# Where four small projections stand: first products with their results kept in DRAM, or last products beside the gate

## The chip, the cores and the metric

The kernel runs on one core of a Trainium2 chip. The metric is the device time of one execution in microseconds (us), the median of several runs. Within a core, TensorE (PE) multiplies, VectorE (DVE), ScalarE (ACT) and GpSimd (POOL) do elementwise work, and SyncE (SP) and ScalarE issue the DMAs used here. Each engine takes its instructions in the order in which they were built.

## The reference

One layer of a hybrid decoder block over 256 tokens and 2048 features, in float32:

```python
h = rmsnorm(x, norm_mix_g)
u = h @ w_in                       # 12288 columns in ten parts
ya = b * conv3(c * xa) * silu(za)  # short convolution, 1024 wide
yb = hgrn2(q, f, iv) * silu(og)    # gated linear recurrence, 1024 wide
m = sigmoid(ga) * (ya @ w_a_out) + sigmoid(gb) * (yb @ w_b_out)
x = x + m @ w_o
gate = sigmoid(rmsnorm(x, ple_norm_g) @ w_ple_gate)
x = x + gate * (p @ w_ple_proj)    # p: 256 tokens x 256, w_ple_proj: 256 x 2048
return rmsnorm(x, final_norm_g)
```

The term `p @ w_ple_proj` depends on inputs alone, so it can be computed at any time before the last sum.

## The kernel before, in words

**Products.** Every float32 operand is split into a high and a low part (`hi` is the value in the matmul's format, `lo = value - hi`), and every product is three matmuls: high by high, high by low, low by high (`product`, L842 to L844). The weights stream in as chunks of 128 x 1024 (512 KB), one chunk per *step*. A step is two k-blocks by two token halves by three matmuls, so 12 matmuls of 512 columns. `split(pos)` makes one step's high part on ScalarE (L119, tile `whi`) and low part on VectorE (L120, `wlo`). Activations are put into their high and low parts by `put` (L156 and L157: `xh`, `xl`).

**Groups.** Steps are gathered in groups by output columns (512 at a time): 24 groups of `w_in` (eight steps each), A and B (four steps each, after each `gb`), O0 to O3 (`w_o`, eight steps) and PG0 to PG3 (`w_pg`, eight steps). The projection of p is PP0 to PP3 (`w_pp`, one step each). Before, PP0 and PP1 stand between O3 and PG0, PP2 follows PG0, and PP3 follows PG1. PG3 is written out apart, at the end, in three pieces.

**PSUM.** `bank("g")` has four banks in rotation and each group takes two, so a group can begin when the epilogue of the group two before it has read its banks.

**Epilogues.** Each group has a generator (`ep_f`, `ep_o`, `ep_pp`, `ep_pg` and so on) that runs in pieces: `advance()` runs every active one up to its next `yield`, once per step. `ep_o` adds the product to x, turns the result (from tokens by features to features by tokens) through DRAM (`turned`: four DMAs out, one back, a transpose on VectorE), and puts it as the operand `x1T` of the PG groups. `ep_pp` copies its two banks to a tile `pw` (L612, ScalarE), which `ep_pg` multiplies with the gate.

**Order.** Two things set it: the main loop over `steps`, which splits weights three steps ahead (`ahead`, `LEAD`) and loads four more (`AHEAD`); and a scheduler that, when the kernel is built, orders each engine's instructions from that program. `tc.issue_after` and `tc.keep_in_program_order` bind it. Raw weights have three buffers of two steps each (`raw`, bufs=3), and split weights four (`wp`), with six more in a pool `late` from PG0 on. Nearly all DMAs are issued on SyncE's queue in order; a DMA that waits holds up those behind it. Eight DMAs may be under way; the next waits for the landing of the one eight before.

**Start.** x comes in transposed as eight pieces (`xT`, 256 KB), between the first six weight chunks, all on SyncE's queue; `prm` (36 KB of gains) is on ScalarE's. Eight warm-up matmuls on a zeroed tile run before the first product.

Of the kernel before, what the change touches and what calls it, by code (L numbers as in the profile page):

```python
# [15 lines left out]
P = 128  # L16
# [7 lines left out]
CW = 512  # L24
PLE = 256
EPS = 1e-6
WARM = 8
LB_FLOOR = 1e-30
LB_MAX = 1.0 - 1e-6
SCAN = 64  # L30
# [14 lines left out]
def hybrid_kernel(ctx, tc, xT, x, pT, prm, gfin, masks, w_in, w_a, w_b, w_o, w_pg, w_pp, out):  # L45
# [28 lines left out]
    def nm(s):  # L74
        uid[0] += 1
        return f"{s}_{uid[0]}"

    def t4(tag="t4", bufs=None):
        bufs = bufs or {"tmp1": 8, "tmp2": 5, "tmp3": 5}[state["tmp"]]
        return pools[state["tmp"]].tile([P, 1024], F32, tag=tag, bufs=bufs, name=nm(tag))  # L80
# [12 lines left out]

    def load(pos):
        w, g, c = stream[pos]
        nch = w.shape[2]
        key = (id(w), g, c // 2)
        if key not in loaded:
            raw = wp.tile([P, 2, 2 * CW], F32, tag="raw", bufs=3, name=nm("raw"))
            loaded[key] = raw  # L100
            if nch == 1 or FIRST <= pos < FIRST + 4:
                for i in range(min(nch, 2)):
                    nc.sync.dma_start(out=raw[:, i, :], in_=w[g, :, c + i, :])
            elif pos >= FIRST:
                nc.sync.dma_start(out=raw, in_=w[g, :, c : c + 2, :])
        return loaded[key]

    def split(pos, halves=(0, 1)):
        w, g, c = stream[pos]
        src = load(pos)[:, c % 2, :]  # L110

        pool, n = (pools["late"], 6) if (pos - state.get("late", len(steps))) % 10 < 6 and "late" in state else (wp, 4)
        if pos not in parts:
            parts[pos] = tuple(
                pool.tile([P, 2 * CW], F32R, tag=tag, bufs=n, name=nm(tag)) for tag in ("whi", "wlo")
            )
        hi, lo = parts[pos]
        s = slice(halves[0] * CW, (halves[-1] + 1) * CW)
        a = nc.scalar.activation(out=hi[:, s], in_=src[:, s], func=AF.Copy)  # L119
        v = nc.vector.tensor_tensor(  # L120
            out=lo[:, s], in0=src[:, s], in1=hi[:, s].bitcast(F32), op=ALU.subtract
        )
        state["splits"] = (a.ins, v.ins)


    prm_t = const.tile([P, PRM_N], F32, name="prm_t")
    nc.scalar.dma_start(out=prm_t, in_=prm)

    if PAD_CONST:
        nc.gpsimd.memset(const.tile([P, PAD_CONST], F32, name="pad"), 0.0)  # L130
# [14 lines left out]
    def operand(pool, tag, n):  # L145

        return tuple(pool.tile([P, n, T], F32R, tag=tag + x, bufs=1, name=nm(tag + x)) for x in "hl")
# [459 lines left out]
            state["rstd2"] = rsqrt_of(tot, NT, D, "r2")  # L607

    def ep_pp(j, psum):
        pw = t4("pw", 2)  # L610
        for t in range(NT):
            nc.scalar.activation(out=pw[:, t * CW : (t + 1) * CW], in_=psum[t], func=AF.Copy)  # L612
        state["pw", j] = pw
        yield

    def ep_pg(j, psum):
        xs, pw, gt = state["x"], state["pw", j], t4()
# [63 lines left out]
        "f": ep_f, "q": ep_q, "iv": ep_iv, "og": ep_og, "c": ep_c, "xa": ep_xa, "za": ep_za, "b": ep_b,  # L681
        "ga": ep_ga, "gb": ep_gb, "A": ep_a, "B": ep_bb, "O": ep_o, "PG": ep_pg, "PP": ep_pp,
    }
    groups = []
    for n, (kind, j) in enumerate(IN_ORDER):
        groups.append((kind, j, w_in, n, "hT"))
        if kind == "gb":
            groups.append(("A", j, w_a, j, "yaT"))
            groups.append(("B", j, w_b, j, "ybT"))
    groups += [("O", j, w_o, j, "mT") for j in range(4)]  # L690
    groups.append(("PP", 0, w_pp, 0, "pT"))
    for j in range(4):
        if j < 3:
            groups.append(("PP", j + 1, w_pp, j + 1, "pT"))
        groups.append(("PG", j, w_pg, j, "x1T"))
    steps = []
    active, done = [], 0
    for gi, (kind, j, w, g, op) in enumerate(groups):
        for c in range(w.shape[2]):
            stream.append((w, g, c))  # L700
            steps.append((gi, c))

    last_group = len(steps) - w_pg.shape[2]


    state["hT"] = operand(big, "x", KT)
    LEAD, AHEAD = 3, 4
    TOKENS, NORM = 6, 10
    FIRST = 6
    xraw = [t4() for _ in range(4)]  # L710
    for c in range(KT // 2):
        n = 2 * (c % 2)
        nc.sync.dma_start(
            out=xraw[c // 2].rearrange("p (k t) -> p k t", k=4)[:, n : n + 2, :],
            in_=xT[:, 2 * c : 2 * c + 2, :],
        )
        if c < FIRST:
            raw, w = load(c)[:, c % 2, :], stream[c][0][0, :, c, :]
            for s in (slice(0, CW), slice(CW, 2 * CW)) if c == 0 else (slice(0, 2 * CW),):
                nc.sync.dma_start(out=raw[:, s], in_=w[:, s])  # L720


    warm = pools["tmp1"].tile([P, 4, P], F32, tag="both", bufs=1, name="warm")
    nc.vector.memset(warm, 0.0)
    warm = warm.rearrange("p h t -> p (h t)").bitcast(mybir.dt.bfloat16)[:, :CW]
    wb = bank("s")
    for _ in range(WARM):
        nc.tensor.matmul(wb, warm[:, :P], warm, start=True, stop=True)
# [64 lines left out]
        g = state["gfin"] = pools["tmp3"].tile([P, D], F32, name="gfin_t")  # L793
        nc.sync.dma_start(out=g, in_=gfin.partition_broadcast(P))

    def load_p():
        pr = t4()[:, : 2 * T]
        nc.sync.dma_start(out=pr.rearrange("p (k t) -> p k t", k=2), in_=pT)
        state["pT"] = operand(pools["tmp3"], "p", 2)
        hi, lo = (v.rearrange("p k t -> p (k t)") for v in state["pT"])  # L800
        nc.scalar.activation(out=hi, in_=pr, func=AF.Copy)
        nc.vector.tensor_tensor(out=lo, in0=pr, in1=hi.bitcast(F32), op=ALU.subtract)

    def third_part():

# [8 lines left out]
        state["ss3"] = sc(12, "ss3", 1)  # L814
        nc.gpsimd.memset(state["ss3"].rearrange("p (t j) -> p t j", t=NT)[:, :, 5:6], EPS)

    def step(e, free=False):

        with ExitStack() as order:
            for i in state["splits"] if done < len(steps) and not free else ():  # L820
                order.enter_context(tc.issue_after(i))
            try:
                next(e)
            except StopIteration:
                active.remove(e)
# [10 lines left out]

        return LEAD + min(max(pos - (last_group - 20), 0) // 4, 5)

    def product(psum, op, k, t, hi, lo, first, last):

        oh, ol = (x[:, k, t * P : (t + 1) * P] for x in op)
        nc.tensor.matmul(psum, oh, hi, start=first, stop=False)  # L842
        nc.tensor.matmul(psum, oh, lo, start=False, stop=False)  # L843
        nc.tensor.matmul(psum, ol, hi, start=False, stop=last)  # L844

    psum = None
    for pos, (gi, c) in enumerate(steps[:last_group]):
        kind, j, w, g, opname = groups[gi]
        nch = w.shape[2]
        if kind == "PG" and j == 0 and c == 0:  # L850
            close_pool("m")
            open_pool("late", "left")
            state["late"] = done
        while done < min(pos + 1 + ahead(pos), len(steps)):
            if done < 2:
                for i in range(2):
                    put_x(2 * done + i)
                    split(done, (i,))
            else:
                for k in range(2 * done, min(2 * done + 2, KT)):  # L860
                    put_x(k)
                split(done)
            done += 1
        if pos == 4:
            begin()
        if 0 <= pos - NORM < 4:
            add_squares(pos - NORM)
        if pos == NORM + 3:
            norm_of_x()
        if pos == NORM + 4:  # L870
            active.append(ep_f(0, waiting))
            step(active[-1])
            nc.sync.dma_start(out=mask_t, in_=masks)
        if c == 0:
            psum = [bank("g") for _ in range(NT)]
        hi, lo = parts.pop(pos)
        for i in range(2):
            k = 2 * c + i
            s = slice(i * CW, (i + 1) * CW)
            for t in range(NT):  # L880
                product(psum[t], state[opname], k, t, hi[:, s], lo[:, s], k == 0, k == 2 * nch - 1)


        if kind == "PP":
            advance()
        for q in range(done, min(done + AHEAD, len(steps)) if pos >= FIRST else 0):
            load(q)
        if 0 <= pos - TOKENS < 4:
            load_tokens(pos - TOKENS)
        if kind != "PP":  # L890
            advance()
        if kind == "O" and j == 0 and c == nch - 3:
            finish()
            third_part()
        if kind == "O" and j > 0 and c == 1:
            residual(j)
        if kind == "O" and j in (1, 2) and c == 4:
            (load_p, load_gfin)[j - 1]()
        if c == nch - 1:
            if kind == "f" and j == 0:  # L900

                waiting = psum
                for n in ("yaT", "ybT"):
                    state[n] = operand(pools["branch"], n, DC // P)
            if kind == "ga" and j == 0:
                finish()
                second_part()
            if kind == "O" and j == 0:
                state["x1T"] = operand(big, "x", KT)
            if kind == "f" and j == 0:  # L910
                continue
            active.append(epilogues[kind](j, psum))
            step(active[-1], kind == "O" and j == 3)

# [94 lines left out]
```

## Time and profile before

| | |
|---|---|
| time, median of 3 runs (lowest to highest) | 836.47 us (836.06 to 836.76) |
| the profiled execution's own time | 836.98 us |
| its span, first to last instruction | 835.2 us |
| TensorE busy (matmuls) | 822.8 us, 99% of the span |
| TensorE weight loads | 684.1 us, 82% |
| VectorE busy | 529.3 us, 63% |
| ScalarE busy | 434.2 us, 52% |
| GpSimd busy | 91.9 us, 11% |
| DMA | 183.01 MB, mean 219 GB/s |
| first product of the program | 6.2 us after the span's start |

The profile shows one execution. Times within it are counted from the span's start. A timeline row gives start, duration, engine, line, operation, output and inputs, and in brackets the idle time of the engine before it and what ended that. TensorE's matmuls overlap their neighbours, so their spacing from start to start tells their rate, not their duration. The row of a stretch gives, behind the busy times of five engines, the granted clock of TensorE, the busy share of the DMA engines and the GB/s.

### The profile page before, as it was taken

The page shows a single profiled execution, that of the slowest core. Times are in us where ns is not written, and L with a number is a line of the kernel's source. Part 1 is how long each engine was busy: PE and PEld are TensorE (multiplying, and loading weights), DVE is VectorE, ACT ScalarE, POOL GpSimd, SP SyncE. Part 2 cuts the span into 40 slices and gives each one's busy share as a digit, 9 for nine tenths or more (in the row PEclk, how much of TensorE's full clock was granted, in tenths as well). Part 3 has the DMA queues.
Part 4 walks back from the last instruction along what each step waited for, and adds up shares of the span by engine and source line. Part 5 has one row for each costly group of instructions (what it writes and reads, how often), then busy time and mean ns, then how long its engine had stood idle before and what let it go on. Part 6 is the DMA issues. An engine that isn't in the chain of part 4 may idle for free.

```text
span 835.2 us, 9807 instructions
## 1 busy us (share of the span) xinstructions
PE 822.8 (99%) x3752; PEld 684.1 (82%) x3752; DVE 529.3 (63%) x600; ACT 434.2 (52%) x563; POOL 91.9 (11%) x76
## 2 busy tenths in 40 slices
PE   8999999999999999999999999999999999999995
PEld 6888888888888888888888888888888888878885
DVE  6557678777684687777655455545546566576722
ACT  7566654545564654545544443543543555475623
POOL 1000054100000153100001001001001000001110
PEclk9999999999999999999999999999999999999998
DMA  9977554747775555648656556655655888685702
GB/s 330 368 238 259 197 182 175 235 166 245 260 249 202 179 177 184 217 151 296 207 188 228 195 196 232 221 188 186 236 196 182 301 272 303 222 320 216 261 1 101
DMA packets 39792, 183.01 MB, mean 219 GB/s; under 512 B 4544, under 2 KB 13760, under 8 KB 21824
## 3 DMA queue, kind: packets, MB, share of 16 engines
q1 hardware_dynamic: 39312, 181.81, 62.8%
q8 instruction: 29, 0.48, 0.2%
q10 hardware_dynamic: 432, 0.56, 0.2%
q14 instruction: 19, 0.16, 0.1%
HBM read 170.82 MB, written 11.53 MB: 218 GB/s over the span
## 4 chain that ended last, share of the span: by engine, by line
PE 96%; issue 1%; ACT 1%; DVE 0%; DMA 0%; POOLq 0%; POOL 0%; DVEq 0%; ACTq 0%
PE g L842 31%; PE g L844 31%; PE g L843 31%; PE s L328 1%; DMA prm_t<-in_prm 0%; PE s L437 0%; PE s L450 0%; PE s L449 0%; PE s L448 0%; ACT whi L119 0%; ACT xs L663 0%; ACT t L593 0%; DVE wlo L120 0%; DVE xl L157 0%; ACT t L646 0%
## 5 line engine op out<-in xcount | busy, mean ns | idle before, releaser
L120 DVE TENSOR_TENSOR wlo<-raw,whi 128x1024 fp32r<-128x1024 f32 (+1 forms) x294 | 361.5, 1234 | 258.5 <-ACT whi L119 257.6
L119 ACT ACTIVATE whi<-raw 128x1024 fp32r<-128x1024 f32 (+1 forms) x294 | 308.1, 1053 | 340.8 <-PE g L844 292.3
L842 PE MATMUL g<-whi,xh 128*128 128x512 f32 (+1 forms) x912 | 353.0, 388 | 2.0 <-ACT whi L119 1.2
L843 PE MATMUL g<-wlo,xh 128*128 128x512 f32 (+1 forms) x912 | 352.2, 386 | 0.0
L844 PE MATMUL g<-whi,xl 128*128 128x512 f32 (+1 forms) x912 | 352.0, 386 | 0.0
L842 PEld LDWEIGHTS g<-whi,xh 128*128 128x128 f32 x912 | 171.8, 189 | 37.2 <-ACT whi L119 2.1
L844 PEld LDWEIGHTS g<-whi,xl 128*128 128x128 f32 x912 | 171.7, 188 | 34.4
L843 PEld LDWEIGHTS g<-wlo,xh 128*128 128x128 f32 x912 | 171.9, 188 | 34.1 <-DVE wlo L120 0.2
L843 PE MATMUL g<-wlo,mh 128*128 128x512 f32 x128 | 49.6, 389 | 0.0
L842 PE MATMUL g<-whi,mh 128*128 128x512 f32 x128 | 49.5, 389 | 0.0
L844 PE MATMUL g<-whi,ml 128*128 128x512 f32 x128 | 49.5, 389 | 0.0
L573 POOL TENSOR_TENSOR t<-ga,gb 128x512 f32<-128x512 f32 x8 | 14.1, 1787 | 249.1 <-DVE gb L569 249.1
L842 PEld LDWEIGHTS g<-whi,mh 128*128 128x128 f32 x128 | 24.0, 188 | 5.0
L843 PEld LDWEIGHTS g<-wlo,mh 128*128 128x128 f32 x128 | 24.0, 188 | 5.0
L374 POOL TENSOR_TENSOR t<-b 128x512 f32<-128x512 f32 x10 | 20.9, 2086 | 65.3 <-DMA raw<-in_w_in 33.6
L844 PEld LDWEIGHTS g<-whi,ml 128*128 128x128 f32 x128 | 24.0, 188 | 4.9
L356 POOL TENSOR_TENSOR X<-t,kT 128x256 f32<-128x256 f32 x12 | 14.1, 1177 | 99.4 <-ACT t L370 57.7
L842 PE MATMUL g<-whi,yaTh 128*128 128x512 f32 x64 | 24.9, 389 | 0.0
L843 PE MATMUL g<-wlo,yaTh 128*128 128x512 f32 x64 | 24.9, 389 | 0.0
L844 PE MATMUL g<-whi,yaTl 128*128 128x512 f32 x64 | 24.9, 389 | 0.0
L842 PE MATMUL g<-whi,ybTh 128*128 128x512 f32 x64 | 24.9, 389 | 0.0
L843 PE MATMUL g<-wlo,ybTh 128*128 128x512 f32 x64 | 24.9, 389 | 0.0
(148 smaller groups left out, 555.9 us busy)
## 6 DMA issues: line engine op xcount, KB each, us to landing
raw<-in_w_in SPq DMA_DIRECT2D x91, 1024.0 KB, 4.9
raw<-in_w_o SPq DMA_DIRECT2D x16, 1024.0 KB, 6.5
raw<-in_w_pg SPq DMA_DIRECT2D x16, 1024.0 KB, 5.5
turn<-t SPq DMA_DIRECT2D x72, 128.0 KB, 2.8
t<-turn SPq DMA_DIRECT2D x18, 512.0 KB, 5.3
raw<-in_w_a SPq DMA_DIRECT2D x8, 1024.0 KB, 4.9
raw<-in_w_b SPq DMA_DIRECT2D x8, 1024.0 KB, 5.0
raw<-in_w_in SPq DMA_DIRECT2D x9, 512.0 KB, 7.8
```

Source lines behind the costliest of these rows:

```text
L119: a = nc.scalar.activation(out=hi[:, s], in_=src[:, s], func=AF.Copy)
L120: v = nc.vector.tensor_tensor(out=lo[:, s], in0=src[:, s], in1=hi[:, s].bitcast(F32), op=ALU.subtract)
L328: nc.tensor.matmul(bk[:, s], X[:, 0, h, :], X[:, 1, h, :], start=True, stop=True)
L356: eng.tensor_tensor(out=xv[:, w, :, :, half, :], in0=ev[:, :, blk, :, half, :], in1=src[:, :, blk, :, half, :], op=ALU.mult,)
L374: nc.gpsimd.tensor_tensor(out=er, in0=br, in1=ref, op=ALU.subtract)
L573: nc.gpsimd.tensor_tensor(out=spread(m, t), in0=blocks(ga[:, s]), in1=blocks(gb[:, s]), op=ALU.add)
L842: nc.tensor.matmul(psum, oh, hi, start=first, stop=False)
L843: nc.tensor.matmul(psum, oh, lo, start=False, stop=False)
L844: nc.tensor.matmul(psum, ol, hi, start=False, stop=last)
```

## The change

The four PP groups become the first groups of the program. Their operand p is loaded first, on SyncE's queue, while the first `w_pp` chunk comes in two halves on ScalarE's queue. `prm` moves to SyncE's queue. p is put by VectorE alone (`put_p`), into the memory that `yaT` takes later. `ep_pp` copies its banks and writes the copy to DRAM (`kept`); `load_projection` reads it back into `pw` during each PG group. The step-and-group list is now made at the top, the raw buffers are shared by pairs of steps (`pos // 2`), the first step's products are in an order of their own, there are ten warm-up matmuls on a tile zeroed to half the width, the token loads and the norm of x move by two positions, and the exemption of O3's first epilogue piece from `issue_after` goes.

```diff
-WARM = 8
+WARM = 10
...
+    def load_first(pos, eng, pieces):
+        w, g, c = stream[pos]
+        for i in range(pieces):
+            s = slice(i * (2 * CW // pieces), (i + 1) * (2 * CW // pieces))
+            eng.dma_start(out=load(pos)[:, pos % 2, s], in_=w[g, :, c, s])
...
+    groups += [("PP", j, w_pp, j, "pT") for j in range(4)]
     for n, (kind, j) in enumerate(IN_ORDER):
...
-    groups.append(("PP", 0, w_pp, 0, "pT"))
-    for j in range(4):
-        if j < 3:
-            groups.append(("PP", j + 1, w_pp, j + 1, "pT"))
-        groups.append(("PG", j, w_pg, j, "x1T"))
+    groups += [("PG", j, w_pg, j, "x1T") for j in range(4)]
...
-    TOKENS, NORM = 6, 10
+    TOKENS, NORM = 8, 12
...
+    load_first(0, nc.scalar, 2)
+    praw = t4()[:, : 2 * T]
+    nc.sync.dma_start(out=praw.rearrange("p (k t) -> p k t", k=2), in_=pT)
+    load_first(1, nc.sync, 1)
     prm_t = const.tile([P, PRM_N], F32, name="prm_t")
-    nc.scalar.dma_start(out=prm_t, in_=prm)
+    nc.sync.dma_start(out=prm_t, in_=prm)
...
     def ep_pp(j, psum):
-        pw = t4("pw", 2)
+        pw, d = t4(), dram.tile([P, 1024], F32, tag="kept", bufs=4, name=nm("kept"))
         for t in range(NT):
             nc.scalar.activation(out=pw[:, t * CW : (t + 1) * CW], in_=psum[t], func=AF.Copy)
-        state["pw", j] = pw
+        state["kept", j] = d
         yield
+        yield
+        nc.sync.dma_start(out=d, in_=pw)
...
     for c in range(KT // 2):
+        if c + 2 < FIRST:
+            load_first(c + 2, nc.sync, 1)
         ... one piece of xT, nc.sync ...
-        if c < FIRST:
-            ... one w_in chunk, nc.sync ...
...
+    def put_p(k):
+        hi, lo = (z[:, k, :] for z in state["pT"])
+        src = praw[:, k * T : (k + 1) * T]
+        nc.vector.tensor_copy(out=hi, in_=src)
+        nc.vector.tensor_tensor(out=lo, in0=src, in1=hi.bitcast(F32), op=ALU.subtract)
+
+    def load_projection(j):
+        pw = state["pw", j] = t4("pw", 2)
+        nc.sync.dma_start(out=pw, in_=state["kept", j])
...
-            if done < 2:
+            if done == 0:
                 for i in range(2):
-                    put_x(2 * done + i)
+                    put_p(i)
                     split(done, (i,))
             else:
-                for k in range(2 * done, min(2 * done + 2, KT)):
+                for k in range(2 * (done - 4), min(2 * (done - 4) + 2, KT)) if done >= 4 else ():
                     put_x(k)
                 split(done)
...
+            for n in ((0,), (2,), (1,)) if pos == 0 and i == 0 else ((0, 1, 2),):
+                for t in range(NT):
+                    product(psum[t], state[opname], k, t, hi[:, s], lo[:, s], k == 0, k == 2 * nch - 1, n)
...
+        if kind == "PG" and c == 4:
+            load_projection(j)
+            if j == 2:
+                load_projection(3)
...
-            step(active[-1], kind == "O" and j == 3)
+            step(active[-1])
```

More of the change, by code (lines that the diff above doesn't have):

```diff
@@ L95, in load @@
         w, g, c = stream[pos]
-        nch = w.shape[2]
-        key = (id(w), g, c // 2)
-        if key not in loaded:
+        if pos // 2 not in loaded:
             raw = wp.tile([P, 2, 2 * CW], F32, tag="raw", bufs=3, name=nm("raw"))
-            loaded[key] = raw
-            if nch == 1 or FIRST <= pos < FIRST + 4:
-                for i in range(min(nch, 2)):
+            loaded[pos // 2] = raw
+            if FIRST <= pos < FIRST + 4:
+                for i in range(2):
                     nc.sync.dma_start(out=raw[:, i, :], in_=w[g, :, c + i, :])
@@ L105, in load @@
                 nc.sync.dma_start(out=raw, in_=w[g, :, c : c + 2, :])
-        return loaded[key]
+        return loaded[pos // 2]
+    def load_first(pos, eng, pieces):
[3 more added lines that the diff above has]
+            eng.dma_start(out=load(pos)[:, pos % 2, s], in_=w[g, :, c, s])
     def split(pos, halves=(0, 1)):
         w, g, c = stream[pos]
-        src = load(pos)[:, c % 2, :]
+        src = load(pos)[:, pos % 2, :]
         pool, n = (pools["late"], 6) if (pos - state.get("late", len(steps))) % 10 < 6 and "late" in state else (wp, 4)
@@ L123, in split @@
         state["splits"] = (a.ins, v.ins)
+    groups = []
+    groups += [("PP", j, w_pp, j, "pT") for j in range(4)]
+    for n, (kind, j) in enumerate(IN_ORDER):
+        groups.append((kind, j, w_in, n, "hT"))
+        if kind == "gb":
+            groups.append(("A", j, w_a, j, "yaT"))
+            groups.append(("B", j, w_b, j, "ybT"))
+    groups += [("O", j, w_o, j, "mT") for j in range(4)]
+    groups += [("PG", j, w_pg, j, "x1T") for j in range(4)]
+    steps = []
+    active, done = [], 0
+    for gi, (kind, j, w, g, op) in enumerate(groups):
+        for c in range(w.shape[2]):
+            stream.append((w, g, c))
+            steps.append((gi, c))
+    last_group = len(steps) - w_pg.shape[2]
+    LEAD, AHEAD = 3, 4
+    TOKENS, NORM = 8, 12
+    FIRST = 6
+    load_first(0, nc.scalar, 2)
+    praw = t4()[:, : 2 * T]
+    nc.sync.dma_start(out=praw.rearrange("p (k t) -> p k t", k=2), in_=pT)
+    load_first(1, nc.sync, 1)
     prm_t = const.tile([P, PRM_N], F32, name="prm_t")
-    nc.scalar.dma_start(out=prm_t, in_=prm)
+    nc.sync.dma_start(out=prm_t, in_=prm)
     if PAD_CONST:
@@ L683, in hybrid_kernel @@
     }
[L684 to L690, printed above, removed]
-    groups.append(("PP", 0, w_pp, 0, "pT"))
-    for j in range(4):
-        if j < 3:
-            groups.append(("PP", j + 1, w_pp, j + 1, "pT"))
-        groups.append(("PG", j, w_pg, j, "x1T"))
[L696 to L703, printed above, removed]
     state["hT"] = operand(big, "x", KT)
-    LEAD, AHEAD = 3, 4
-    TOKENS, NORM = 6, 10
-    FIRST = 6
+    for n in ("yaT", "ybT"):
+        state[n] = operand(pools["branch"], n, DC // P)
+    state["pT"] = tuple(z[:, :2, :] for z in state["yaT"])
     xraw = [t4() for _ in range(4)]
     for c in range(KT // 2):
+        if c + 2 < FIRST:
+            load_first(c + 2, nc.sync, 1)
         n = 2 * (c % 2)
@@ L716, in hybrid_kernel @@
         )
-        if c < FIRST:
-            raw, w = load(c)[:, c % 2, :], stream[c][0][0, :, c, :]
-            for s in (slice(0, CW), slice(CW, 2 * CW)) if c == 0 else (slice(0, 2 * CW),):
-                nc.sync.dma_start(out=raw[:, s], in_=w[:, s])
     warm = pools["tmp1"].tile([P, 4, P], F32, tag="both", bufs=1, name="warm")
-    nc.vector.memset(warm, 0.0)
-    warm = warm.rearrange("p h t -> p (h t)").bitcast(mybir.dt.bfloat16)[:, :CW]
+    nc.vector.memset(warm[:, :2, :], 0.0)
+    warm = warm[:, :2, :].rearrange("p h t -> p (h t)").bitcast(mybir.dt.bfloat16)
     wb = bank("s")
@@ L794, in load_gfin @@
         nc.sync.dma_start(out=g, in_=gfin.partition_broadcast(P))
[L796 to L802, printed above, removed]
+    def put_p(k):
[6 more added lines that the diff above has]
+        nc.sync.dma_start(out=pw, in_=state["kept", j])
     def third_part():
@@ L815, in third_part, with step @@
         nc.gpsimd.memset(state["ss3"].rearrange("p (t j) -> p t j", t=NT)[:, :, 5:6], EPS)
-    def step(e, free=False):
+    def step(e):
         with ExitStack() as order:
-            for i in state["splits"] if done < len(steps) and not free else ():
+            for i in state["splits"] if done < len(steps) else ():
                 order.enter_context(tc.issue_after(i))
@@ L837, in ahead, with product @@
         return LEAD + min(max(pos - (last_group - 20), 0) // 4, 5)
-    def product(psum, op, k, t, hi, lo, first, last):
+    def product(psum, op, k, t, hi, lo, first, last, which=(0, 1, 2)):
         oh, ol = (x[:, k, t * P : (t + 1) * P] for x in op)
-        nc.tensor.matmul(psum, oh, hi, start=first, stop=False)
-        nc.tensor.matmul(psum, oh, lo, start=False, stop=False)
-        nc.tensor.matmul(psum, ol, hi, start=False, stop=last)
+        for n in which:
+            a, b = ((oh, hi), (oh, lo), (ol, hi))[n]
+            nc.tensor.matmul(psum, a, b, start=first and n == 0, stop=last and n == 2)
     psum = None
@@ L879, in hybrid_kernel @@
             s = slice(i * CW, (i + 1) * CW)
-            for t in range(NT):
-                product(psum[t], state[opname], k, t, hi[:, s], lo[:, s], k == 0, k == 2 * nch - 1)
-        if kind == "PP":
+            for n in ((0,), (2,), (1,)) if pos == 0 and i == 0 else ((0, 1, 2),):
+                for t in range(NT):
+                    product(psum[t], state[opname], k, t, hi[:, s], lo[:, s], k == 0, k == 2 * nch - 1, n)
+        if kind == "PG" and j == 0 and c < 2:
             advance()
@@ L889, in hybrid_kernel @@
             load_tokens(pos - TOKENS)
-        if kind != "PP":
+        if kind != "PG" or j or c >= 2:
             advance()
@@ L896, in hybrid_kernel @@
             residual(j)
-        if kind == "O" and j in (1, 2) and c == 4:
-            (load_p, load_gfin)[j - 1]()
+        if kind == "O" and j == 2 and c == 4:
+            load_gfin()
+        if kind == "PG" and c == 4:
+            load_projection(j)
+            if j == 2:
+                load_projection(3)
         if c == nch - 1:
@@ L902, in hybrid_kernel @@
                 waiting = psum
-                for n in ("yaT", "ybT"):
-                    state[n] = operand(pools["branch"], n, DC // P)
             if kind == "ga" and j == 0:
```

## The prediction

> **What bounds it now.** I read the page first, then the timelines of the two places that the change touches, the start and the seam between the group O3 and the group PG0.
>
> ```profile
> span 835.2 us, 9807 instructions
> PE 96%; issue 1%; ACT 1%; DVE 0%; DMA 0%; POOLq 0%; POOL 0%; DVEq 0%; ACTq 0%
> ```
>
> The chain that ended last is TensorE for 96%, so the time is the number of products times their spacing, plus what TensorE waits. The change keeps every product. Only waits and the slow first products can move.
>
> ```profile
> 6.22 1.22 PE L842 MATMUL g<-whi,xh 128*128 128x512 f32 x2 [1.17 <-ACT whi L119]
> 10.23 0.57 PE L842 MATMUL g<-whi,xh 128*128 128x512 f32 x1
> 10.63 0.40 PE L843 MATMUL g<-wlo,xh 128*128 128x512 f32 x1
> 13.63 0.39 PE L844 MATMUL g<-whi,xl 128*128 128x512 f32 x1
> 13.85 0.62 PE L842 MATMUL g<-whi,xh 128*128 128x512 f32 x2
> ```
>
> This is TensorE's timeline at the start. Products begin at 6.22. The first ten stand 0.43 us apart (to 10.23), the others 0.227 (13.63 to 13.85). A step has 12 products, so the 25th product, the first of step 2, starts at 13.85. From there TensorE runs without a break to the seam. So the question at the front is: when does the 25th product start afterwards?
>
> ```profile
> 731.66 0.39 PE L844 MATMUL g<-whi,pl 128*128 128x512 f32 x1
> 732.91 0.50 PE L842 MATMUL g<-whi,xh 128*128 128x512 f32 x1 [0.87 <-ACT pw L612]
> ...
> 732.29 1.06 ACT L612 ACTIVATE pw<-g 128x512 f32<-128x512 f32 x2
> 735.15 2.97 ACT L119 ACTIVATE whi<-raw 128x1024 fp32r<-128x1024 f32 x3
> ```
>
> The seam, TensorE then ScalarE. PG0 starts 1.25 us after the last product of PP1 instead of 0.23: 1.02 us lost. It waits for ScalarE to copy PP0's result out of PSUM, because tag "g" has four banks and every group takes two. This wait is the key to the forecast: two PP groups fill all four banks, and the third user must wait for a copy.
>
> **The front: gain that cannot arrive.** The first products need p (256 KB) and half a w_pp chunk (256 KB), the same bytes as now (x, w_in), but issued at once on two queues instead of 0.44 us apart, and they need no value of prm. VectorE's copy and subtraction of p take the place of ScalarE's 0.91 us. I put the first product at 5.5 to 5.9, so 0.3 to 0.7 us earlier. The shorter memset (0.48 us for 512 columns, now 256) and ten warm-up products of 0.43 us (4.3 us) end near 5.5, so the break before the first product shrinks. At the slow spacing the two steps PP0 and PP1 end by 15.9, and by about 13.3 if the spacing drops at 9 to 10 us, since step 1's weights split near 10.7. All of this is cover for what comes next, and I count it at nothing.
>
> **The front: the new wait.** PP2 (step 2) needs PP0's two banks, so ScalarE's copies at the line `pw[...] <- psum[t]` of ep_pp. In the built order of the changed kernel ScalarE does, in this order: the splits of steps 0 to 3, x's pairs 0 and 1, step 4's split, x's pair 2, step 5's split, and only then the four copies of PP0 and PP1. It is one in-order engine, so PP2 waits for step 5's weights to land. In the built order there are in front of and with those weights: p 256 KB, six weight chunks 3072 KB, three x pieces 768 KB, prm 36 KB: 4132 KB. Before, the same 4132 KB were in when the sixth x piece landed:
>
> ```profile
> 7.42 0.51 SPq L713 DMA_DIRECT2D t<-in_xT  x1
> ...
> t<-in_xT SPq DMA_DIRECT2D x1, 256.0 KB, 8.7
> ```
>
> Issued at 7.42, 8.7 us to landing: 16.1. Then step 5's split (three took 2.97, so 0.99), the copy (1.06 for the pair; alone 0.59, the mean of the eight) and 0.04 to TensorE, as at 732.87 to 732.91: 16.1 + 0.99 + 0.59 + 0.04 = 17.7. The 25th product starts at 17.7 instead of 13.85: **3.9 us lost.** Bounds for the landing: 17.4 (where step 5's weights land now, behind 512 KB more) and 12.4 (4.23 MB at the 410 GB/s of the row below, from 2.0 us on). I take 16.1, since it is the same bytes through the same engines. The Trainium skill, "DMA: Bandwidth & Descriptors", section "Issuing engines are not separate DMA queues", says that queues of several engines share the same 16 DMA engines and that issuing from two saves issue time alone; by it the second queue moves nothing here, as in the sum by equal bytes, and this trace, with prm alone on the second queue, cannot test it.
>
> After 17.7 the front holds. SyncE's queue now has the four `kept` writes (512 KB each) among the weight loads, and each waits for its copy. The worst is step 6 and 7's load behind the first write: issued near 18.7, landed by 24, wanted split by 28.6. Step 8's load is behind the third write (copy near 23.7, after eight pieces of x at 0.43 each): landed near 28, wanted at 34. Step 4 wants PP2's banks at 23.1, copied at 22.8 and 23.7, the second wanted at 23.8. Cost nothing; if this cover were gone, each us late is a us lost.
>
> **The seam.** PP0 and PP1 no longer stand there, so PG0's banks are free and the 1.02 us are **gained**. But the same two groups gave 24 x 0.227 = 5.4 us of cover to O3's way through DRAM: add, copy, turn out, turn back, transpose, put. PG0's 7th step reads what it puts.
>
> ```profile
> 726.54 1.27 DVE L157 SCALAR_TENSOR_TENSOR xl<-t,prm_t,xh 128x256 fp32r<-128x256 f32 x3
> 728.86 0.68 DVE L585 TENSOR_TENSOR xs<-xs,g 128x512 f32<-128x512 f32 x1
> 742.47 1.24 DVE L198 STREAM_TRANSPOSE t<-t 128x1024 f32<-128x1024 f32 x1
> 745.86 1.66 DVE L157 SCALAR_TENSOR_TENSOR xl<-t,prm_t,xh 128x256 fp32r<-128x256 f32 x4
> ```
>
> O3's last product ends at 726.4. If nothing changed, the first low part would be ready at 745.86 + 0.42 = 746.3. PG0 started at 726.4 wants it at 726.4 + 74 x 0.227 = 743.2, so 3.1 us stall. In the built order, however, the second add follows the first at once, no longer behind the puts of O2 and a split (at 726.5 instead of 728.86). ScalarE then makes a split, copy, square, copy (1.04 + 0.63 + 0.80 + 0.63), so the turn goes out at 729.5 instead of 730.2, and one split less stands between transpose and puts (1.2). That makes 746.3 - 0.7 - 1.2 = 744.4: 1.2 stall. The two loads that slowed the turn now are issued earlier; 512 KB of `pw` join them. Both ends 0 and 3.1; I take 0.6, between 0 and 1.2. Net of the seam: -0.4, from -1.0 to +2.1.
>
> **The rest.** Projection weights (2 MB) leave the end and 2 MB of `pw` come back there: the same bytes. The 2 MB written at the front are in spare DMA time after 20 us. The eight copies (4.7 us of ScalarE) leave an end where TensorE waited for them only at the seam. The tail after the last product is unchanged. All nothing.
>
> **Sum:** 3.9 - 0.4 = +3.5 on a span of 835.2: 838.7. The profiled execution took 836.98, 0.51 above the median of the runs, so the median goes from 836.47 to about **840.0**.
>
> **Rivals.**
> (1) *The slow spacing returns.* TensorE idles from about 13.3 to 17.7. The trace shows what idling can do:
>
> ```profile
> 10.60:13.80 3.20, 3.20 (x15) 2.61 (x14) 2.90 (x6) 3.10 (x7) 0.00 (x0) 1.00 1.03 410
> 826.50:829.70 3.20, 0.00 (x0) 0.00 (x0) 1.56 (x5) 1.39 (x4) 0.56 (x1) 1.00 0.00 0
> 829.90:835.00 5.10, 0.00 (x0) 0.00 (x0) 0.40 (x1) 0.58 (x1) 0.00 (x0) 0.50 0.56 207
> ```
>
> These are stretches with the granted clock third from last: 1.00 for 3.4 us after the last product (826.3), 0.50 from 829.8 on. The drop came 3.5 us after the end; the 1.0 us break at the seam left the spacing at 0.23. My break of 4.4 us is longer by 0.9 only, and it shrinks to 1.8 if PP0 and PP1 run at 0.43 throughout (24 products from 5.6, to 15.9); so this is less likely than not. Price: 2.0 us (ten products 0.2 too long, as at the start) to 3.7 (slow from the warm-up at 1.45 to 10.6, 8.0 busy us of 0.43, so 18.7 products); 2.9 in the middle: 842.9. Chance 0.27. The Trainium skill, "TensorE: Matmul & The Clock Gate", section "What's actually happening", has the clock halved after a whole idle window of about 3.4 us, the windows running freely; an estimate from that page is that a break of 4.4 us holds a whole one in about 3 cases of 10. The tail of this trace agrees, with 3.5 us.
> (2) *Not slower: the data come early.* If two queues fill the DMA engines from 2 us on, step 5's weights land at 12.4 and not 16.1; PP2 starts at 14.0, 0.2 late, and the seam gives 1.0: 835.6. The point where it decides is a landing at 13.2. Against it: before, the DMAs ran at 238 GB/s from 5.1 to 6.2 us with work queued, which a second queue does not explain away. Chance 0.12, with landings up to 14.9 (838.1).
> (3) *The seam stalls in full*, 3.1 us, since the latencies of the turn stay: 3.9 - 1.0 + 3.1 = +6.0, 842.5. For it: DMA stays as busy there. Against: the built order drops the work ahead of the second add. Chance 0.12.
>
> **Numbers.** Forecast 0.46 with a range of its own from 838.3 (landing at 15.0, free seam) to 841.6 (landing at 17.0, seam +0.3); rivals 0.27, 0.12, 0.12; 0.03 for anything else. The range 837.5 to 843.7 leaves out most of rival 2 below, and above it the dear end of rivals 1 and 3. What a measurement here tells from no change is about 0.2%, 1.67 us. Slower by more: forecast, rivals 1 and 3: 0.85. Within: nearly all of rival 2, 0.12. Faster by more (below 834.8) needs a landing before 12.4 and a free seam: 0.03.
>
> **What would show it.** TensorE's timeline has a gap of about 4 us before its 25th product, ended by ScalarE's copy in ep_pp, and step 5's split stands right ahead of that copy at 16 to 17 us. Products after it at 0.43 mean rival 1. At the seam the last product of O3 is followed by PG0 within 0.25 us, and any gap lies 16 us later, ended by a put. I am wrong if the 25th product starts before 15, or if the copies run before step 5's weights land.

## The result, and the profile after

| | before | after |
|---|---|---|
| median of 5 runs each, one chip (lowest to highest), us | 836.47 (836.06 to 836.81) | 840.18 (839.48 to 840.42) |
| ratio, 95% interval | | 1.0043 (1.0028 to 1.0057) |
| the profiled execution's own time, its span | 836.98, 835.2 | 840.28, 838.5 |
| the 25th product starts at | 13.85 | 16.37 |
| the last product starts at | 826.04 | 829.72 |

The changed kernel is slower by 3.7 us, close to the forecast (840.0). The parts of that sum, however, are not those of the forecast. First the page of the changed kernel:

```profile
span 838.5 us, 9821 instructions
PE 96%; issue 1%; DMA 1%; ACT 1%; DVE 0%; SPq 0%; POOLq 0%; POOL 0%; ACTq 0%
```

TensorE is still the chain for 96%, so the loss must be in its waits or its spacing. Its timeline at the start (start, duration, operation; in brackets the idle time and what ended it):

```profile
5.24 0.73 PE L859 MATMUL g<-whi,yaTh 128*128 128x512 f32 x2 [0.31 <-DVE yaTl L812]
...
11.86 0.39 PE L859 MATMUL g<-whi,yaTl 128*128 128x512 f32 x1
16.37 0.80 PE L859 MATMUL g<-whi,yaTh 128*128 128x512 f32 x1 [4.12 <-ACT t L643]
16.96 0.63 PE L859 MATMUL g<-wlo,yaTh 128*128 128x512 f32 x1
17.39 0.63 PE L859 MATMUL g<-whi,yaTl 128*128 128x512 f32 x1
...
20.80 0.56 PE L859 MATMUL g<-wlo,yaTh 128*128 128x512 f32 x1
21.20 0.39 PE L859 MATMUL g<-whi,yaTl 128*128 128x512 f32 x1
21.42 0.39 PE L859 MATMUL g<-whi,yaTh 128*128 128x512 f32 x1
```

Two things are to be seen. The 25th product waits 4.12 us for the copy of ep_pp, and starts 2.52 us later than before. And behind the break the products stand 0.43 us apart until 21.20: eleven of them take 4.83 us where 11 x 0.227 = 2.50 would do, another 2.33 us. The rows by stretch (five busy times, granted clock, DMA share, GB/s) say why:

```profile
4.10:10.80 6.70, 5.81 (x23) 3.52 (x22) 5.07 (x9) 4.45 (x7) 0.53 (x1) 1.00 1.02 367
10.90:14.30 3.40, 1.35 (x6) 0.77 (x5) 2.85 (x6) 2.87 (x6) 0.00 (x0) 1.00 1.01 397
14.40:17.70 3.30, 1.33 (x3) 1.14 (x4) 2.69 (x4) 3.21 (x7) 0.00 (x0) 0.50 0.86 322
17.80:21.10 3.30, 3.30 (x9) 2.60 (x8) 2.87 (x7) 3.25 (x8) 0.00 (x0) 0.50 1.00 274
21.20:30.00 8.80, 8.80 (x40) 7.29 (x39) 5.02 (x13) 6.12 (x11) 0.00 (x0) 1.00 0.99 375
```

The granted clock is halved in the middle of the break and comes back at 21.14. What held the copy is in ScalarE's timeline:

```profile
13.79 0.89 ACT L187 ACTIVATE xh<-t,prm_t 128x256 fp32r<-128x256 f32 x2
14.78 1.06 ACT L124 ACTIVATE whi<-raw 128x1024 fp32r<-128x1024 f32 x1
15.74 2.04 ACT L643 ACTIVATE t<-g 128x512 f32<-128x512 f32 x4
```

Step 5's split runs at 14.78, and PP0's copies follow it. The load that it needs was issued at 6.95 and landed 7.7 us later, at 14.67:

```profile
6.95 0.43 SPq L111 DMA_DIRECT2D raw<-in_w_in  x1
...
raw<-in_w_in SPq DMA_DIRECT2D x1, 512.0 KB, 7.7
```

ScalarE itself was busy with the two pieces of x before it until 14.68, so the landing and the engine held the split to the same time. TensorE, then VectorE, at the seam:

```profile
741.94 0.39 PE L859 MATMUL g<-whi,ml 128*128 128x512 f32 x1
742.17 0.39 PE L859 MATMUL g<-whi,xh 128*128 128x512 f32 x1
```

```profile
741.94 1.28 DVE L616 TENSOR_TENSOR xs<-xs,g 128x512 f32<-128x512 f32 x2
...
755.23 1.25 DVE L229 STREAM_TRANSPOSE t<-t 128x1024 f32<-128x1024 f32 x1
756.40 1.18 DVE L125 TENSOR_TENSOR wlo<-raw,whi 128x1024 fp32r<-128x1024 f32 x1
757.51 1.66 DVE L188 SCALAR_TENSOR_TENSOR xl<-t,prm_t,xh 128x256 fp32r<-128x256 f32 x4
```

PG0 follows O3's last product by 0.23 us: the 1.02 us are gained. The first low part of x is there at 757.51 + 0.42 = 757.9, and PG0's 75th product wants it at 742.17 + 74 x 0.227 = 759.0, so nothing stalls.

The spans' difference: +2.52 (the wait), +2.33 (slow products), -1.02 (seam), -0.38 (the tail behind the last product, 8.88 us before and 8.50 after), and -0.15 that small steps leave: +3.30. The medians differ by 3.71, because the profiled execution of the kernel before took 0.51 more than its median and that of the changed kernel 0.10. The start of the kernel before varies: in e6_before_spare_banks (below), which begins with the same instructions, the clock is full at 9.45 instead of 10.59 and the 25th product starts at 13.14 instead of 13.85. So the 2.52 us are counted against a late start of the kernel before.

### The profile page after: what moved, and what is told of

The parts are those of the page before. It is cut to its first block, busy times and chain, and to the rows that moved or that the text cites. A ratio compares the mean times of both kernels' runs of the same rounds, so it can differ in the third digit from the quotient of the medians.

```text
span 838.5 us, 9821 instructions
## 1 busy us (share of the span) xinstructions
PE 823.8 (98%) x3754; PEld 684.2 (82%) x3754; DVE 530.5 (63%) x602; ACT 434.8 (52%) x561; POOL 92.3 (11%) x76
## 4 chain that ended last, share of the span: by engine, by line
PE 96%; issue 1%; DMA 1%; ACT 1%; DVE 0%; SPq 0%; POOLq 0%; POOL 0%; ACTq 0%
PE g L859 93%; PE s L359 1%; DMA raw<-in_w_pp 1%; PE s L468 0%; ACT whi L124 0%; PE s L480 0%; PE s L481 0%; PE s L479 0%; ACT xs L696 0%; DVE wlo L125 0%; ACT t L679 0%; SPq L111 0%; ACT xh L187 0%; DVE t L675 0%; POOLq L1024 0%
## 5 line engine op out<-in xcount | busy, mean ns | idle before, releaser
L859 PE MATMUL g<-whi,yaTh 128*128 128x512 f32 x80 | 32.3, 406 | 4.8 <-ACT t L643 4.1
L859 PE MATMUL g<-wlo,yaTh 128*128 128x512 f32 x80 | 32.1, 403 | 0.2 <-DVE wlo L125 0.2
L859 PE MATMUL g<-whi,yaTl 128*128 128x512 f32 x80 | 31.7, 398 | 0.0
```

Source lines behind the costliest of these rows:

```text
L859: nc.tensor.matmul(psum, a, b, start=first and n == 0, stop=last and n == 2)
```

## The experiments

The theory: PP2 has no free banks, the copy that frees them stands behind step 5's split, and the break this makes also halves the clock. The first rival: the results' way through DRAM, 2.1 MB written at the start and read back at the end, is the cost. The second: the clock is lost for another reason than the break. Times are medians, with lowest to highest; in the same runs the kernel before had 836.43 (e1 to e4), 836.35 (e5 to e8) and 836.76 us (e9 and e10). The end of a label says what the run changes.

### Other banks for PP2 and PP3 (e1_spare_banks)

```diff
-            psum = [bank("g") for _ in range(NT)]
+            psum = [bank("s" if kind == "PP" and j > 1 else "g") for _ in range(NT)]
```

> The changed kernel with PP2 and PP3 in two pairs of the banks of tag s, which nothing else uses so early. Theory A (the loss is PP2's wait for PP0's banks, 2.5 us, and the slow products after the break, 2.3 us): the break before the 25th product goes, it starts near 12.1 instead of 16.4, the spacing stays at 0.23; then step 6 is next to be late, since its weights are still behind the first kept write on SyncE's queue and its split behind nine pieces of x, about 1.7 us. Sum 840.2 - 4.3 - 2.3 + 1.7 = 835.3. Theory B (the loss is the 4 MB of extra DMA traffic): the break may go but the time stays near 840.

Measured: 835.97 us (835.53 to 837.44), ratio to before 0.9995 (0.9986 to 1.0004). The break and the slow products are gone: the 25th product starts at 12.17, and the clock is 1.00 from 4.59 to 830.62. That is 4.20 + 2.33 us, but only 4.2 us of it are left at the end, since new waits have come at steps 6, 8 and 10 (1.1, 0.4 and 0.5 us beyond the spacing, from the starts of the products):

```profile
24.43 0.50 PE L859 MATMUL g<-wlo,xh 128*128 128x512 f32 x1 [0.53 <-DVE wlo L125]
...
36.25 0.50 PE L859 MATMUL g<-wlo,xh 128*128 128x512 f32 x1 [0.18 <-DVE wlo L125]
```

Its SyncE queue shows where these weights were:

```profile
16.50 0.33 SPq L647 DMA_DIRECT2D kept<-t  x1
16.93 1.20 SPq L101 DMA_DIRECT2D raw<-in_w_in  x2
18.22 0.91 SPq L647 DMA_DIRECT2D kept<-t  x2
19.23 1.40 SPq L101 DMA_DIRECT2D raw<-in_w_in  x2
```

The loads of steps 6 to 13 stand behind `kept` writes, which wait for copies. In the changed kernel the same queue costs nothing, because TensorE starts step 6 there 6.4 us later (29.61 against 23.17): one delay covers the other.

### The kept writes on GpSimd's queue as well (e7_writes_apart)

```diff
-        nc.sync.dma_start(out=d, in_=pw)
+        nc.gpsimd.dma_start(out=d, in_=pw)
```

> As e1_spare_banks, with the four kept writes issued on GpSimd's queue instead of SyncE's. e1 came out at 835.97 with waits of 1.3, 0.4 and 0.4 us at steps 6, 8 and 10, whose loads were issued at 16.9 and 19.2 behind kept writes. If the place on SyncE's queue makes these waits, the loads are issued near 12.5 and 15, and the time is 833.9. If the bytes of the writes make them, the waits stay: 835.5 to 836.

Measured: 834.29 us (834.14 to 834.70), ratio 0.9976 (0.9967 to 0.9985). SyncE's queue is now this:

```profile
12.91 2.90 SPq L101 DMA_DIRECT2D raw<-in_w_in  x4
```

The loads go out from 12.91 on, and the waits at steps 6, 8 and 10 are gone. The last product starts at 823.07, 2.13 us earlier than with the spare banks alone: 2.04 of it are the three waits, 0.09 an earlier 25th product (12.08). The medians differ by 1.68 only. In the profiled runs the tail behind the last product makes up for the rest (9.06 us here, 8.49 there). Over the twelve traces this tail is 8.49 to 8.54 in eight and 8.84 to 9.06 in four, and why was not shown.

### Work in the break (e2_fill_break, e8_half_fill)

```diff
+        if kind == "PP" and j == 2:
+            fill = bank("s")
+            for _ in range(FILL):
+                tc.keep_in_program_order(nc.tensor.matmul(fill, warm[:, :P], warm, start=True, stop=True))
```

FILL is 16 in the first and 8 in the second.

> The changed kernel with 16 matmuls on zeros (512 columns, 0.215 to 0.23 us each, 3.6 us together) between PP1 and PP2, so that TensorE is busy in most of the break, and nothing else is changed. Theory A: PP2 starts at 16.4 as before, but the granted clock stays at 1.00 and the spacing after the break at 0.23: 2.3 us less, 837.9. Rival: if the slow products hide behind later waits or the drop has another cause, 840.2 as without.

Measured: 837.93 us (837.76 to 838.53), ratio 1.0020 (1.0011 to 1.0029). TensorE's timeline:

```profile
12.15 3.63 PE L895 MATMUL s<-warm 128*128 128x512 bf16 x16
16.59 0.50 PE L860 MATMUL g<-whi,yaTh 128*128 128x512 f32 x1 [0.81 <-ACT t L644]
16.93 0.39 PE L860 MATMUL g<-wlo,yaTh 128*128 128x512 f32 x1
17.16 0.40 PE L860 MATMUL g<-whi,yaTl 128*128 128x512 f32 x1
```

The 25th product comes as late as in the changed kernel (16.59 against 16.37), yet the spacing is 0.23 behind it. So the slow products come from the idle time, they are worth 840.18 - 837.93 = 2.25 us, and the second rival falls; the wait alone is what is left.

> As e2_fill_break, with 8 matmuls on zeros instead of 16: a break of about 2.4 us is left. If the clock drops only after a whole idle window of 3.4 us, it never drops here: 837.9 and a mean clock of 0.997 in every run, as in e2. If a window that is idle for the greater part is enough (in the changed kernel it dropped 2.1 us after the last product), it drops in some runs or all: 838.3 to 840.2, mean clocks of 0.993 to 0.996 among them.

Measured: 838.73 us (837.67 to 839.93), in two groups: four runs from 837.67 to 838.01 at a mean clock of 0.996 to 0.997, four from 839.44 to 839.93 at 0.995. With an idle stretch of 2.0 us (14.29 to 16.29 in the profiled run), half of the runs lost the clock. So a stretch of 3.4 us without any work is not needed. The profiled run was one of those that kept it (the third number from the end is the clock):

```profile
12.70:16.00 3.30, 1.59 (x8) 0.50 (x6) 3.29 (x7) 3.17 (x5) 0.53 (x1) 1.00 1.03 402
```

### One queue for the first weights (e3_one_queue)

```diff
-    load_first(0, nc.scalar, 2)
+    load_first(0, nc.sync, 2)
```

> The changed kernel with the two halves of the first weight chunk issued on SyncE's queue too. Step 5's weights landed at 14.7 where I had forecast 16.1. If the second queue gave these 1.4 us, they land near 16.1 now and PP2 starts near 17.8: 841.6. If it gave issue time alone (two issues of 0.44 us), they land by 15.1 to 15.6, PP2 starts by 17.3 at most, and the time is 840.2 to 841.1.

Measured: 841.07 us (840.09 to 841.51), ratio 1.0053 (1.0040 to 1.0065). Step 5's weights land at 15.65 instead of 14.67, and the 25th product follows:

```profile
12.07 0.39 PE L859 MATMUL g<-whi,yaTl 128*128 128x512 f32 x1
17.35 0.80 PE L859 MATMUL g<-whi,yaTh 128*128 128x512 f32 x1 [4.89 <-ACT t L643]
```

The second queue moved that landing by 0.98 us between these two traces. Nine traces have the loads of the changed kernel's start, and this landing scatters from 14.34 to 14.95, so the gain is 0.7 to 1.3. The issue of p is 0.90 us later here (1.64 instead of 0.74), the time in which SyncE's queue issues the two halves, and that is enough to explain the gain. A gain of the whole 1.4 us, with the landing at 16.1, was not seen.

### Without the way through DRAM (e4_no_round_trip)

```diff
-        nc.sync.dma_start(out=d, in_=pw)
...
-        nc.sync.dma_start(out=pw, in_=state["kept", j])
+        nc.gpsimd.memset(pw, 0.0)
```

The last term of the reference's second sum is left out.

> The changed kernel without the four writes of kept and the four reads of pw (pw is zeroed on GpSimd instead, so the gate's term is left out). Theory A: PP2's wait and the break stay as they are, the time is 839.7 to 840.3. Theory B (traffic, and the writes among the loads on SyncE's queue): 1 to 3 us faster, 837 to 839.

Measured: 839.44 us (839.35 to 840.43), ratio 1.0038 (1.0024 to 1.0051). The break is there as before, and so are twelve products at 0.43 us (the granted clock is 0.50 from 14.76 to 21.58). The median lies 0.26 us below the forecast of theory A, because three of the five runs are at a mean clock of 0.995; of the changed kernel's runs two of five were. At equal mean clock the two agree: 839.35 to 839.44 against 839.48 and 839.72 at 0.995, 840.25 and 840.43 against 840.18 to 840.42 at 0.993. So 4.2 MB more or less of traffic is not the cause, and the first rival falls.

### The copies ahead of the splits (e5_reordered)

```diff
+            copied = nc.scalar.activation(out=pw[:, t * CW : (t + 1) * CW], in_=psum[t], func=AF.Copy)
+        state["kept", j], state["copied"] = d, copied.ins
...
+                with ExitStack() as order:
+                    if "copied" in state and done < 8:
+                        order.enter_context(tc.issue_after(state["copied"]))
                     ... put_x and split as before ...
```

> The changed kernel, banks as they were, with the splits of steps 4 to 7 and their pieces of x queued on ScalarE behind the copies of the PP group before them, so that no copy stands behind a weight load. Theory A: the same break goes by another way, the 25th product starts near 12.1 with the clock at 1.00, and since the copies are made by 12 us the first kept write no longer holds up step 6's load behind itself (issue near 13.4 instead of 16.5): 833.6 to 834.5. Rival: if it is the number of banks itself or the traffic and not the order on ScalarE, 839 to 840.

Measured: 834.34 us (834.04 to 834.86), ratio 0.9976 (0.9967 to 0.9985). ScalarE's timeline:

```profile
9.98 1.06 ACT L124 ACTIVATE whi<-raw 128x1024 fp32r<-128x1024 f32 x1 [0.89 <-DMA raw<-in_w_pp]
10.95 1.07 ACT L643 ACTIVATE t<-g 128x512 f32<-128x512 f32 x2
11.90 0.91 ACT L187 ACTIVATE xh<-t,prm_t 128x256 fp32r<-128x256 f32 x2
12.74 1.06 ACT L124 ACTIVATE whi<-raw 128x1024 fp32r<-128x1024 f32 x1
```

PP0's copies run at 10.95 instead of 15.74, ahead of the splits of steps 4 and 5. The 25th product, on TensorE, waits for nothing:

```profile
12.08 0.39 PE L859 MATMUL g<-whi,yaTh 128*128 128x512 f32 x1
```

With the same banks, bytes and queues, the break is gone, and the clock stays at 1.00 from 6.04 to 828.65. So the cost was the place of two copies in the order of one engine. One wait of 0.7 us is left, at step 8.

### That order with the kept writes apart (e9_reordered_apart)

The edit of e7_writes_apart on top of e5_reordered.

> The reordered start together with the kept writes on GpSimd's queue. Theory A (what is left of waits in the reordered kernel is step 8's, 0.6 us, and comes from a load that stood behind a kept write on SyncE's queue): that wait goes and nothing takes its place, 833.5 to 834.0 us, with the spacing at 0.227 us from the first product that has it to the end. Alternative: the wait at step 8 is the order of the splits on ScalarE and VectorE, which the queues don't change: 834.3, as the reordered kernel alone, with the wait at step 8 still there.

Measured: 834.48 us (834.18 to 835.03), ratio 0.9972 (0.9960 to 0.9983). The wait at step 8 is gone, but step 6's split now comes late instead (ScalarE has its weights at 21.18), with 0.5 us; the last product starts at 823.61 instead of 823.73. That the queue held step 8 is shown; that nothing would take its place was wrong. It is no better than e5_reordered or e7_writes_apart, which beat both kernels.

### The warm-up as it was (e10_warm8)

```diff
-WARM = 10
+WARM = 8
...
-    nc.vector.memset(warm[:, :2, :], 0.0)
+    nc.vector.memset(warm, 0.0)
```

> The changed kernel with the warm-up as in the kernel before: eight matmuls and the whole tile zeroed. Theory A (two matmuls more and half a memset less are worth nothing, because the 25th product waits for step 5's weights whenever the first product starts): 839.5 to 840.4, the same as the changed kernel, and the 25th product at 16.3 to 16.5. Alternative (the start counts, since a later first product leaves a shorter break and so a full clock): the first ten products at the slow spacing, the break under 3 us, no slow products behind it, 837.5 to 838.

Measured: 840.58 us (839.43 to 841.15), ratio 1.0041 (1.0029 to 1.0054), the same as the changed kernel's 1.0043. The first product starts at 5.23 instead of 5.24. The 25th starts at 16.65, because step 5's weights landed at 14.95 in this trace, and the time is 0.2 above the forecast. The two matmuls more and the shorter memset are worth nothing that can be measured.

### The kernel before, with spare banks (e6_before_spare_banks)

```diff
-            psum = [bank("g") for _ in range(NT)]
+            psum = [bank("s" if kind == "PP" else "g") for _ in range(NT)]
```

> The kernel before, with the four PP groups in banks of tag s where they stand, so that PG0 needn't wait for PP0's copy. My reading of the seam: 1.0 us less, 835.4, PG0 starts 0.23 us after PP1. Rival: the wait hides another (O3's put, a load), and PG0 or its 7th step stalls for it: 836.0 to 836.4.

Measured: 835.16 us (834.55 to 835.66), ratio 0.9986 (0.9977 to 0.9995), so 1.2 us less. Its TensorE timeline at the seam:

```profile
730.91 0.39 PE L844 MATMUL s<-whi,pl 128*128 128x512 f32 x1
731.14 0.39 PE L842 MATMUL g<-whi,xh 128*128 128x512 f32 x1
```

PG0 follows PP1 by 0.23 us. The seam's wait was the banks, and it could be had without moving anything.

## Why the prediction was right in its total and wrong in its parts

**The mechanism at the front** was right: PP2 waits for PP0's banks, the copies stand behind step 5's split, and that waits for its weights. e1_spare_banks takes away the need for the banks and e5_reordered the place of the copies, and with either the break goes.

**The start**: the first product came at 5.24 (5.5 to 5.9 was forecast), and TensorE was done with 24 products at 12.25 (13.3 to 15.9), since the clock was already full at 4.07. As said, none of it arrived in the changed kernel; it only made the break begin earlier. Where the copies no longer wait it does arrive: 12.08 in e5_reordered.

**The size of the wait** was not as forecast. The term "the 25th product starts at 17.7 ... 3.9 us lost" measured 2.52. Of the step 16.1 + 0.99 + 0.59 + 0.04, the last three terms measured 16.37 - 14.67 = 1.70 against 1.62; the landing is the term that failed, 14.67 instead of 16.1. It was taken from equal bytes, as if two queues moved nothing. e3_one_queue shows that the second queue was worth 0.98 us of the 1.43 (0.7 to 1.3 with the scatter of that landing); the other 0.45 stay unexplained (with one queue, too, the landing was 15.65). The sum also left out that ScalarE is busy until 14.68. Had the weights come earlier still, its own work would have held PP2: without the 0.53 us that it idled between step 3's split at 10.43 and the copies, PP2 would have started near 15.8, as an estimate, and not at the 14.0 of rival 2. The Trainium skill, "DMA: Bandwidth & Descriptors", section "Issuing engines are not separate DMA queues", grants a second issuing engine the issue time alone; the run agrees, with 0.90 us of issue and 0.98 us of landing. The prediction read it as "the second queue moves nothing here": at the head of a queue that everything waits for, the issue time is the gain.

**The slow products** were rival 1, with a chance of 0.27 and left out of the sum. They came, at 2.33 us by the profile and 2.25 by e2_fill_break, within the price of 2.0 to 3.7 that the rival had. The step that failed is "The drop came 3.5 us after the end", read as the time that a drop takes. In this break the clock fell at 14.31, 2.06 us after the last product ended (12.25), with TensorE busy for 1.35 of the 3.41 us up to that point. The Trainium skill, "TensorE: Matmul & The Clock Gate", section "What's actually happening", asks for a whole idle window; the estimate of 3 in 10 in the prediction came from that, and here the trace and e8_half_fill decide against it.

**The seam**: the gain of 1.02 is as forecast, and e6_before_spare_banks bears it out by itself. The stall of 0.6 measured 0, with 1.0 us to spare. As said there, the second add follows the first at once; but the transpose came 13.06 us after the start of the next group (755.23 from 742.17), against 16.06 before, and the forecast had taken only 0.7 off this stretch. The turn goes out 1.1 us sooner, its four writes land in 4.3 us instead of 5.8, and the transpose starts at the landing instead of 1.0 us behind it, while the way back takes 0.6 more. Rival 3 fell with it.

**Counted at nothing**: the `kept` writes cost nothing in the changed kernel, with the cover that was named, a late TensorE. Without it they cost 2.0 us of waits (e1_spare_banks against e7_writes_apart; 1.7 by the medians). The warm-up was worth nothing (e10_warm8). The tail differed by 0.38 between the two profiled runs.

**The sum**: 3.9 + 0.6 - 1.0 = +3.5 was forecast, and the same three terms measured 2.5 + 0 - 1.0 = +1.5. The slow products (+2.3) and the small terms (-0.5) bring it to the +3.3 of the spans. So the total was met by luck: 2.0 us too much in two terms stood against 2.3 us that the sum had left out. Rival 2, an early landing, was wrong at 12.4, and 14.67 lay inside its stretch of landings (up to 14.9); without the slow products it would have given 837.9, as e2_fill_break did.

**The move itself**: with its order mended (e5_reordered, 834.34) it beats the kernel before by 2.0 us and that kernel with spare banks (835.16, same runs) by 0.8.

## What to carry to other kernels

When a group is moved to where the engines start, look in the built order of each in-order engine for what stands between its last product and the copy that frees its PSUM: a copy that needs nothing can stand behind a split that waits for a load. A break of TensorE has two prices, its length and the products at half the clock behind it; work out both, and take the second as certain for a break of 4 us (all 20 runs of the four kernels with such a break had a mean clock of 0.995 or less). When a delay is removed, look at the queue that it covered, since the next wait is often already there.

## What the runs showed of the hardware

The points at which the granted clock changes lie on a grid of 3.413 us in every trace (4.07, 14.31, 21.14 and 833.51 in the changed kernel: 3, 2 and 238 steps apart), and where that grid lies against the start of the span differs between runs. What decides a drop can be read from the ends of the kernels, where TensorE stops at once. Two runs with spare banks, e7_writes_apart and then e1_spare_banks, each in windows of its grid (the ends are cut by up to 0.1 us; the first number behind the length is TensorE's busy time):

```profile
821.90:825.20 3.30, 1.45 (x13) 1.25 (x11) 0.85 (x2) 0.86 (x3) 0.00 (x0) 1.00 0.00 0
825.30:828.60 3.30, 0.00 (x0) 0.00 (x0) 1.31 (x3) 1.35 (x3) 0.56 (x1) 0.50 0.33 122
```

```profile
823.80:827.20 3.40, 1.68 (x15) 1.48 (x13) 0.85 (x2) 0.73 (x2) 0.00 (x0) 1.00 0.00 0
827.25:830.60 3.35, 0.00 (x0) 0.00 (x0) 1.31 (x3) 1.54 (x4) 0.56 (x1) 1.00 0.28 102
830.65:834.00 3.35, 0.00 (x0) 0.00 (x0) 0.00 (x0) 0.00 (x0) 0.00 (x0) 0.50 0.55 203
```

After a window with 1.45 us of matmuls (1.49 in the whole window) the clock fell; after one with 1.68 it held for one window more. In the break of the changed kernel it fell (1.35 us in the window); in the profiled run of e8_half_fill it held (1.6, from 12.68 to 16.09). All twelve traces fit one limit: the clock falls after a window with less than some 1.5 to 1.6 us of matmuls in its 3.41, so with over 1.8 to 1.9 us idle. By that, as an estimate, a break under 1.8 us never costs the clock, one over 3.9 us always does, and one of 2.0 us does so in about half of the places on the grid, as four runs in eight did. The runs of the changed kernel lie in two groups (839.48 and 839.72 at a mean clock of 0.995, 840.18 to 840.42 at 0.993). That this is one slow window or two was not shown: all profiled runs that lost the clock had two.

The way back asks for more work than keeping the clock does. Windows with 2.24 to 2.50 us of matmuls (the starts of the kernel before, e6_before_spare_banks and e9_reordered_apart) and with 2.05 and 2.08 us (behind the break in e4_no_round_trip and e10_warm8) left it at 0.50, and one with 2.88 us (the start of the changed kernel) brought it to 1.00. The first window behind the changed kernel's drop had 1.35 us of products, so a second slow one followed, and the break of 4.1 us cost 6.8 us at half the clock.
